# Attention weights times values in plain float32, two heads in two column halves of the array

## The chip, the cores and the metric

The kernel runs on one core of a Trainium2 chip. The metric is the device time of one execution in microseconds; three runs of the kernel before gave 1371.66 to 1372.84 us with a median of 1371.97. A core has a matrix engine (TensorE, in the profile PE, its weight loads PEld), a vector engine (DVE), a scalar engine (ACT), a general engine (POOL) and a queue engine that starts transfers (SP). They run side by side and wait for each other through semaphores.

## The reference

One step of a two-layer decoder: a retention layer, then a layer of sliding-window attention with grouped heads. There are 1024 prompt tokens and 8 decode tokens. The attention of the prompt, cut to what matters here:

```python
kk, vv = band(k), band(v)          # key blocks i-1 and i for query block i, 128 tokens each
scores = einsum('bnqkgd,bnskd->bnkgqs', qb, kk) * (SWA_HD ** -0.5)
scores = where(valid, scores - alibi_slopes() * dist, NEG)
p = sink_softmax(scores, sinks)    # softmax with one extra column per head, then dropped
o = einsum('bnkgqs,bnskd->bnqkgd', p, vv)
...
o = o * silu(gate)
return x + o @ w_out
```

There are 16 query heads of width 64 and 2 key/value heads, 8 query heads for each. A block of queries reads its own block of keys and the one before; the first block reads only its own. The change concerns the last product, `o`.

## The kernel before

The matrix engine multiplies a stationary operand (the weights, up to 128 rows by 128 columns) with a moving one, and adds up in PSUM. The kernel wants more precision than its fast float type, `float32r`, gives. So it splits most operands into a rounded part and the rest (`hi` and `lo`, both float32r) and adds three products: hi x hi, hi x lo, lo x hi. The rounded part is made by an ACT copy, the rest by a subtraction, mostly on DVE.

The program has these stages: the projections of the retention layer (to about 700 us with the retention itself), the retention layer's output projection (to about 909 us), keys and values of the attention layer (to about 955 us), the attention units (955 to 1280 us), and the rest of the output projection.

The keys and values are made per block of 128 tokens (`kv_mm`, `kv_ev`, `kv_tr`, `kv_kk`). `kv_ev` scales the values out of PSUM into `vvh` (rounded) and `vvl` (the rest). Both are kept for all eight blocks, 128 columns each, 64 per key/value head. For the last block a further copy, `vo`, is made and written to an output.

A unit of attention is a pair of query heads and a block of queries: 8 pairs by 8 blocks make 64 units. They share out into groups of 3, 3 and 2 blocks (`TG`). A unit has four steps:

- `att_s`: four products of queries and keys (two heads, hi and lo of the keys) into `sc`, then bias, maximum and exponential (DVE, ACT).
- `att_r`: the reciprocal of the sum (DVE) and the scaling of the weights (POOL).
- `att_x`: the weights are transposed on PE in blocks of 128 by 128, four of them in a unit (two in the first block of a sequence, which has one key block), into a PSUM tile `tr` with the columns [key block][head][query]. ACT copies them, rounded, to `pth`, DVE subtracts to get `ptl`.
- `att_o`: the products with the values into the PSUM tile `o`, of which there is one. Its 64 partitions hold the width of a head, its 256 columns are the 128 queries of head 0 and those of head 1. ACT copies each half, times 0.5, into its half of the partitions of `ot`, and POOL multiplies by the gate `gt`.

Around these steps, `fill` puts pieces of the projections of queries and gates (`pair_proj`, lines L1090 to L1092, 384 or 264 columns each), so that PE has other work while the other engines do the softmax of a unit. The main loop at the end of `_trunk` sets this order: `att_s` and `att_r` of unit m+4, a piece of projection, `att_x` of unit m+1, another piece, `att_o` of unit m, another piece. PE runs in exactly the order in which the code is written; for DVE, ACT, POOL and SP the order behind the first units is made by a scheduler from the dependences.

Other lines that the text below speaks of: L1430 and L1432 are small plain float32 products of squares with `hsel` for the norm of the queries (L1432 only in the last group of a pair, with 2 columns of weights); L1601 and L1606 are the scores of the decode tokens, plain float32 with 16 columns of weights; L1643 and L1645 their products with the values; L1380 copies transposed keys of the cache; L103 is the helper of all transposes.

Of the kernel before, what the change touches and what calls it, by code (L numbers as in the profile page):

```python
# [7 lines left out]
F32 = mybir.dt.float32  # L8
F32R = mybir.dt.float32r
AF = mybir.ActivationFunctionType  # L10
ALU = mybir.AluOpType
# [52 lines left out]
def trunk(tc, x_prompt, x_sample, state_ret, cache_k, cache_v, norm_ret, w_in_ret, ret_out_norm,  # L64
          w_out_ret, norm_swa, w_in_swa, q_norm, k_norm, sinks, w_out_swa, c1, c2,
          y_p, y_s, nrp, nrs, nkp, nvp, nks, nvs):
    nc = tc.nc
    ctx = ExitStack()
    with ctx:
        ctx.enter_context(tc.manual_schedule(engines=MS))  # L70
        _trunk(ctx, tc, nc, locals())


def _trunk(ctx, tc, nc, a):
# [7 lines left out]
    nkp, nvp, nks, nvs = a["nkp"], a["nvp"], a["nks"], a["nvs"]  # L82
# [12 lines left out]
    mm = nc.tensor.matmul  # L95
# [6 lines left out]
    def tr(out, in_, ident, start=True, stop=True):  # L102
        nc.tensor.matmul(out, in_, ident, is_transpose=True, start=start, stop=stop)  # L103
# [501 lines left out]
    o = lambda fn, *a: (fn, a)  # L605
# [118 lines left out]
    for h in range(H):  # L724
        t0 = max(t0 + GAP, sets[3 * h + 2].end + 10.0)
        for hf in range(2):
            for b in range(ND):
                d = {}
# [493 lines left out]
    o = 0  # L1222
# [23 lines left out]
    opp = ctx.enter_context(tc.tile_pool(name="opp", bufs=1, space=PSUM))  # L1246
    kvp = ctx.enter_context(tc.tile_pool(name="kvp", bufs=1))
    atp = ctx.enter_context(tc.tile_pool(name="atp", bufs=1))

    kkh = kvp.tile([128, 2, NP], F32R, name="kkh")  # L1250
    kkl = kvp.tile([128, 2, NP], F32R, name="kkl")
    vvh = kvp.tile([128, 8, 128], F32R, name="vvh")
    vvl = kvp.tile([128, 8, 128], F32R, name="vvl")
    kdd = kvp.tile([8, 128], F32, name="kdd")
    vdd = kvp.tile([8, 128], F32, name="vdd")
    rbc = kvp.tile([128, NT], F32, name="rbc")
# [4 lines left out]
    def knorm_a(src, r, n):  # L1261

        kj = atp.tile([128, HD], F32, tag="s", name="kj", bufs=6)
        ss = atp.tile([128, 2], F32, name="kss", bufs=2)
        rk = atp.tile([128, 2], F32, name="krk", bufs=2)
        for g in range(2):
            nc.scalar.activation(kj[:n], src[:, g * 64:g * 64 + 64], AF.Square, scale=r, accum_out=ss[:n, g:g + 1])
        nc.vector.tensor_scalar(ss[:n], ss[:n], 1.0 / HD, EPS, ALU.mult, ALU.add)
        rsq(rk[:n], ss[:n], 2)
        return rk  # L1270

    def knorm_b(out4, src, rk, r, n, dup):

        nc.vector.tensor_scalar(rk[:n], rk[:n], r, None, ALU.mult)
        for g in range(2):
            nc.vector.scalar_tensor_tensor(
                out4[:, g], src[:, g * 64:g * 64 + 64].unsqueeze(1).broadcast_to([n, dup, 64]), rk[:n, g:g + 1],
                kgb[:n].unsqueeze(1).broadcast_to([n, dup, 64]), ALU.mult, ALU.mult)
# [19 lines left out]
    def kv_ev(c):  # L1298
        ps = kvst[c]
        r = r9[:, c:c + 1]  # L1300
        nc.scalar.activation(vvh[:, c, :], ps[:, 128:256], AF.Copy, scale=r)
        rk = knorm_a(ps[:, 0:128], r, 128)
        nc.vector.scalar_tensor_tensor(vvl[:, c, :], ps[:, 128:256], r, vvh.bitcast(F32)[:, c, :],
                                       ALU.mult, ALU.subtract)
        kd = atp.tile([128, 2, 2, HD], F32, tag="s", name="kd", bufs=6)
        knorm_b(kd, ps[:, 0:128], rk, r, 128, 2)
        if c == 7:
            vo = atp.tile([128, 128], F32, tag="s", name="vo", bufs=6)
            nc.scalar.activation(vo, ps[:, 128:256], AF.Copy, scale=r)
            nc.scalar.dma_start(out=nvp[0, 0].rearrange("s g d -> s (g d)"), in_=vo)  # L1310
        kvst[c] = kd

    def kv_tr(c):
# [58 lines left out]
    def dec_cache(hf):  # L1372

        pt = trp.tile([128, 512], F32, name="tr")
        for i in range(4):
            tr(pt[:, i * 128:i * 128 + 128], kcT["c"][:, 4 * hf + i, :], ident)
        return pt
# [107 lines left out]
    for p_ in range(8):  # L1485
        for ti_, (t0_, t1_) in enumerate(TG):
            nch_ = (min(t1_, NP) - t0_) // 128
            for i_ in range(nch_):
                u = Unit()
# [48 lines left out]
    def att_x(u):  # L1538
        hs = (0, 1) if u.c > 0 else (1,)
        pt = trp.tile([128, 512], F32, name="tr")  # L1540
        for hf in hs:
            for j in range(2):
                tr(pt[:, hf * 256 + j * 128:hf * 256 + j * 128 + 128], u.st[:, j, hf * 128:hf * 128 + 128], ident)
        a0 = hs[0] * 256
        pth = atp.tile([128, 512], F32R, name="pth", bufs=2)
        ptl = atp.tile([128, 512], F32R, name="ptl", bufs=2)
        nc.scalar.activation(pth[:, a0:], pt[:, a0:], AF.Copy)
        nc.vector.tensor_tensor(ptl[:, a0:], pt[:, a0:], pth.bitcast(F32)[:, a0:], ALU.subtract)
        u.pt = (pth, ptl)

    def att_o(u):
        p, ti, i, c = u.p, u.ti, u.i, u.c
        if i == 0:
            ots[p, ti] = atp.tile([128, 384], F32, name="ot", bufs=2)
        ot, gt = ots[p, ti], G[p, ti]
        hs = (0, 1) if c > 0 else (1,)
        pth, ptl = u.pt
        po = opp.tile([64, 256], F32, tag="o", name="o")
        vs = slice(u.g * 64, u.g * 64 + 64)
        for hf in hs:  # L1560
            kc = c - 1 + hf
            rs_ = slice(hf * 256, hf * 256 + 256)
            mm(po, vvh[:, kc, vs], pth[:, rs_], start=(hf == hs[0]), stop=False)
            mm(po, vvl[:, kc, vs], pth[:, rs_], start=False, stop=False)
            mm(po, vvh[:, kc, vs], ptl[:, rs_], start=False, stop=(hf == 1))
        cs = slice(i * 128, i * 128 + 128)
        for j in range(2):
            nc.scalar.activation(ot[j * 64:j * 64 + 64, cs], po[:, j * 128:j * 128 + 128], AF.Copy, scale=0.5)
        nc.gpsimd.tensor_tensor(ot[:, cs], ot[:, cs], gt[:, cs], ALU.mult)
        if i == u.nch - 1:  # L1570
            done["o"] += 1
            n = u.nch * 128
            if p < 7:
                nc.scalar.dma_start(out=oscr[p, :, u.t0:u.t0 + n], in_=ot[:, :n])
            else:
                ts_ = slice(u.t0, u.t0 + n)
                nc.scalar.activation(A_hi[:, 7, ts_], ot[:, :n], AF.Copy)
                nc.vector.tensor_tensor(A_lo[:, 7, ts_], ot[:, :n], A_hif[:, 7, ts_], ALU.subtract)
                oready[ti] = True
# [118 lines left out]
    def so_all():  # L1698
        order = [(ft, ti) for ti in range(3) for ft in range(6)] + [(ft, ti) for ft in (6, 7) for ti in range(3)]
        early = []  # L1700

        def start(ft, ti):
            so_ahead(ft // 2 + 1)
            t0, t1 = TG[ti]
            n = t1 - t0
            xr = iop2.tile([128, 384], F32, tag="xr", bufs=2, name="xr2")
            nc.sync.dma_start(out=xr[:, :n], in_=xscr[ft, :, t0:t1])
            nso[0] += 1
            ps = (msp.tile([128, 512], F32, tag="ms", name="pm") if nso[0] % 3 == 0 else
                  pjp.tile([128, 512], F32, tag="pj", name="pj"))  # L1710
            for k in range(7):
                proj(ps[:, :n], so_slots[ft // 2], ft % 2, t0, t1, first=(k == 0), last=False, ks=[k])
                yield 3 * n / 2400.0
            early.append((ft, ti, ps, xr))

        def finish():
            ft, ti, ps, xr = early.pop(0)
            t0, t1 = TG[ti]
            n = t1 - t0
            proj(ps[:, :n], so_slots[ft // 2], ft % 2, t0, t1, first=False, last=True, ks=[7])  # L1720
            yield 3 * n / 2400.0
            yt = io("sq", 2)
            nc.vector.tensor_tensor(yt[:, :n], ps[:, :n], xr[:, :n], ALU.add)
            if pend_y:
                so_y(*pend_y.pop(0))
            pend_y.append((ft, ti, yt))

        for ft, ti in order:
            while early and (oready[early[0][1]] or len(early) == 3):
                while not oready[early[0][1]]:  # L1730
                    yield 1e9
                yield from finish()
            while ti == 2 and not oready[2]:
                yield 1e9
            yield from start(ft, ti)
        while early:
            yield from finish()
        while pend_y:
            so_y(*pend_y.pop(0))
# [6 lines left out]
    def stream():  # L1746
        for p in range(8):
            yield from pair_proj(p)

    ps = stream()  # L1750
    ones = atp.tile([128, 128], F32, tag="s", name="ones", bufs=6)
    nc.gpsimd.memset(ones, 1.0)
    out = so_all()
# [49 lines left out]
    pt = dec_cache(0)  # L1803
# [5 lines left out]
    pt = dec_cache(1)  # L1809
# [10 lines left out]
    fill(ps, 3.0)  # L1820
    att_r(units[3])
    att_x(units[0])
    sk.close()
    src = ps
# [8 lines left out]
    for m in range(NU):  # L1833
        u = units[m]
# [66 lines left out]
```

## Time and profile before

| | |
|---|---|
| three runs, median (lowest, highest) | 1371.97 us (1371.66, 1372.84) |
| profiled execution, span from the first to the last instruction | 1368.6 us |
| mean granted clock of TensorE | 0.987 |
| attention units, stretch 955 to 1280 us: PE busy | 316.16 of 325 us |
| products of `att_o`: records in the trace | 3 x 120, 128 rows x 64 columns of weights, 256 columns moving |
| DVE, `ptl` | 56 of 686 ns, 8 of 412 ns |
| ACT, `pth` | 56 of 595 ns, 8 of 367 ns |
| ACT, `ot` | 128 of 266 ns |

The page of a profile describes one execution. Its times are in microseconds where not marked ns. A group of instructions is written as line, engine, operation, output<-inputs, shapes, count | busy time, mean ns of one | idle time of the engine just before them, and what ended it. A timeline row is the start, the time that the row covers, the engine, the line and the operation, with neighbouring equal instructions merged (x4). Matmuls are pipelined: the recorded duration of one reaches past the start of the next, so the distance from start to start is what one costs in a stream.

### The profile page before, as it was taken

To read this page: it belongs to the slowest core of one execution; us is meant where nothing else is said; L and a number is where in the kernel's file an instruction comes from. 1 tells how busy PE (TensorE), PEld (TensorE's weight loads), DVE (VectorE), ACT (ScalarE), POOL (GpSimd) and SP (SyncE) were. 2 spreads that over 40 slices of the span, in tenths; PEclk is the share of its full clock that TensorE was granted. 3 is DMA by queue.
4 is the path that set the end of the run, shared out by engine and by line. 5 is a ranking of instruction groups with operands and counts; after the bars stand their busy time and mean duration, and the time that the engine had idled before them with its cause. 6 is when DMAs were issued, how large, how long until landed. Compare 5 with 4: busy or idle time off the path is not lost.

```text
span 1368.6 us, 25998 instructions
## 1 busy us (share of the span) xinstructions
PE 1313.7 (96%) x9541; PEld 1251.6 (91%) x9541; DVE 745.5 (54%) x1434; ACT 669.1 (49%) x1690; POOL 760.5 (56%) x886
## 2 busy tenths in 40 slices
PE   6999999999999999897979999998999999999998
PEld 6999999999999999686868889997899999998998
DVE  6943665566556553675752112335576777779321
ACT  5532555555556653675741112244576666667311
POOL 6753656655566753697976553544476666544000
PEclk9999999999999999999989999999999999999999
DMA  6314767667667653665645344442111111112532
GB/s 218 103 59 143 220 211 230 176 214 231 199 215 209 219 156 93 188 176 191 172 150 164 123 154 125 135 131 66 47 50 59 44 47 41 40 34 88 170 84 82
DMA packets 192804, 186.66 MB, mean 136 GB/s; under 512 B 12725, under 2 KB 172525, under 8 KB 192661
## 3 DMA queue, kind: packets, MB, share of 16 engines
q1 hardware_dynamic: 155840, 148.87, 35.9%
q10 hardware_dynamic: 36836, 36.14, 8.3%
q8 instruction: 75, 1.23, 0.4%
q14 instruction: 53, 0.43, 0.1%
HBM read 128.59 MB, written 57.41 MB: 136 GB/s over the span
## 4 chain that ended last, share of the span: by engine, by line
PE 84%; DVE 5%; POOL 4%; DMA 3%; issue 2%; ACT 2%; SPq 0%; ACTq 0%; POOLq 0%; DVEq 0%
PE b L340 7%; PE b L342 7%; PE b L341 7%; PE pj L1090 5%; PE pj L1091 5%; PE pj L1092 5%; PE pj L1141 4%; PE pj L1139 4%; PE pj L1140 4%; PE b L334 4%; PE b L333 4%; PE b L335 4%; PE tr L103 3%; PE S L921 1%; PE S L922 1%
## 5 line engine op out<-in xcount | busy, mean ns | idle before, releaser
L340 PE MATMUL b<-xh,woh 128*128 128x258 f32 x784 | 222.4, 284 | 0.0
L342 PE MATMUL b<-xh,wol 128*128 128x258 f32 x784 | 221.9, 283 | 0.0
L341 PE MATMUL b<-xl,woh 128*128 128x258 f32 x784 | 221.6, 283 | 0.0
L1090 PE MATMUL pj<-A_hi,wh 128*128 128x384 f32 (+1 forms) x512 | 173.0, 338 | 0.0
L1091 PE MATMUL pj<-A_lo,wh 128*128 128x384 f32 (+1 forms) x512 | 165.7, 324 | 0.0
L1092 PE MATMUL pj<-A_hi,wl 128*128 128x384 f32 (+1 forms) x512 | 165.5, 323 | 0.0
L340 PEld LDWEIGHTS b<-xh,woh 128*128 128x128 f32 x784 | 148.2, 189 | 1.2
L341 PEld LDWEIGHTS b<-xl,woh 128*128 128x128 f32 x784 | 148.8, 190 | 0.0
L342 PEld LDWEIGHTS b<-xh,wol 128*128 128x128 f32 x784 | 148.2, 189 | 0.0
L1080 POOL TENSOR_TENSOR wl<-wr,wh 128x1024 fp32r<-128x1024 f32 (+1 forms) x60 | 114.8, 1924 | 46.4 <-DVE wh L1079 22.1
L334 PE MATMUL b<-wol,xh 128*128 128x256 f32 x448 | 126.1, 282 | 1.2 <-DVE wol L224 1.2
L333 PE MATMUL b<-woh,xh 128*128 128x256 f32 x448 | 125.9, 281 | 0.0
L335 PE MATMUL b<-woh,xl 128*128 128x256 f32 x448 | 125.8, 281 | 0.0
L1536 POOL TENSOR_TENSOR s<-s,sm 128x512 f32<-128x512 f32 x64 | 67.7, 1057 | 69.2 <-DVE sm L1535 67.5
L282 POOL TENSOR_TENSOR yl<-yd,yh 128x256 fp32r<-128x256 f32 x64 | 56.3, 879 | 82.0 <-PE od L289 40.3
L1090 PEld LDWEIGHTS pj<-A_hi,wh 128*128 128x128 f32 x512 | 98.0, 191 | 0.2
L1091 PEld LDWEIGHTS pj<-A_lo,wh 128*128 128x128 f32 x512 | 98.0, 191 | 0.0
L1092 PEld LDWEIGHTS pj<-A_hi,wl 128*128 128x128 f32 x512 | 97.4, 190 | 0.0
L224 POOL TENSOR_TENSOR wol<-raw,woh 128x512 fp32r<-128x512 f32 x52 | 68.8, 1331 | 47.8 <-ACT woh L219 46.9
L334 PEld LDWEIGHTS b<-wol,xh 128*128 128x128 f32 x448 | 84.4, 188 | 1.4 <-DVE wol L224 1.4
L333 PEld LDWEIGHTS b<-woh,xh 128*128 128x128 f32 x448 | 84.4, 188 | 0.7
L335 PEld LDWEIGHTS b<-woh,xl 128*128 128x128 f32 x448 | 84.4, 188 | 0.0
(368 smaller groups left out, 3847.0 us busy)
## 6 DMA issues: line engine op xcount, KB each, us to landing
raw<-in_w_in_ret_dram ACTq DMA_DIRECT2D x44, 512.0 KB
st<-in_state_ret_dram SPq DMA_DIRECT2D x64, 256.0 KB
out_dram<-st SPq DMA_DIRECT2D x64, 256.0 KB
wr<-in_w_out_ret_dram SPq DMA_DIRECT2D x32, 512.0 KB
wr<-in_w_in_swa_dram SPq DMA_DIRECT2D x18, 512.0 KB
vb<-vscr SPq DMA_DIRECT2D x64, 128.0 KB
evp<-qks SPq DMA_DIRECT2D x32, 256.0 KB
evx<-vsc SPq DMA_DIRECT2D x32, 256.0 KB
```

The costliest lines, as they stand in the source:

```text
L224: eng.tensor_tensor(lo, src_of(s, name, sub), hi.bitcast(F32), SUB)
L333: mm(dst, xh, wh, start=a and i == 0, stop=False, skip_group_check=True)
L334: mm(dst, xh, wl, start=False, stop=False, skip_group_check=True)
L335: mm(dst, xl, wh, start=False, stop=z, skip_group_check=True)
L340: mm(dst, wh, xh, start=a, stop=False, **sg)
L341: mm(dst, wh, xl, start=False, stop=False, **sg)
L342: mm(dst, wl, xh, start=False, stop=z, **sg)
L1080: lo_eng[0].tensor_tensor(lo[:, js, :], raw[:, i:i + step, :], hi.bitcast(F32)[:, js, :], ALU.subtract)
L1090: mm(ps, hi[:, k, fs], xh[:, k, t0:t1], start=first and k == ks[0], stop=False)
L1091: mm(ps, hi[:, k, fs], xl[:, k, t0:t1], start=False, stop=False)
L1092: mm(ps, lo[:, k, fs], xh[:, k, t0:t1], start=False, stop=last and k == ks[-1])
L1536: nc.gpsimd.tensor_tensor(st[:, :, 0:256], st[:, :, 0:256], sm.unsqueeze(2).broadcast_to([128, 2, 256]), ALU.mult)
```

## The change

The values are kept once, in plain float32 (`vv`), and the transposed weights too (`ptf`). The subtractions that made `vvl` and `ptl` are gone, and so is the extra copy of the last block's values, whose output is now written from `vv`. In `att_o` each key block is multiplied separately for the two heads, with the same 64 columns of values as weights: head 0 writes partitions 0 to 63 of `o`, head 1 partitions 64 to 127. So `o` has 128 partitions and 128 columns, and one ACT copy takes it to `ot`. In the built program the products of `att_o` are marked, before as now, with a tile of 128 rows by 64 columns of the array; before all of them at column 0, now head 0 at column 0 and head 1 at column 64.

```diff
-    vvh = kvp.tile([128, 8, 128], F32R, name="vvh")
-    vvl = kvp.tile([128, 8, 128], F32R, name="vvl")
+    vv = kvp.tile([128, 8, 128], F32, name="vv")
...
-        nc.scalar.activation(vvh[:, c, :], ps[:, 128:256], AF.Copy, scale=r)
+        nc.scalar.activation(vv[:, c, :], ps[:, 128:256], AF.Copy, scale=r)
         rk = knorm_a(ps[:, 0:128], r, 128)
-        nc.vector.scalar_tensor_tensor(vvl[:, c, :], ps[:, 128:256], r, vvh.bitcast(F32)[:, c, :],
-                                       ALU.mult, ALU.subtract)
...
-            vo = atp.tile([128, 128], F32, tag="s", name="vo", bufs=6)
-            nc.scalar.activation(vo, ps[:, 128:256], AF.Copy, scale=r)
-            nc.scalar.dma_start(out=nvp[0, 0].rearrange("s g d -> s (g d)"), in_=vo)
+            nc.scalar.dma_start(out=nvp[0, 0].rearrange("s g d -> s (g d)"), in_=vv[:, 7, :])
...
-        pth = atp.tile([128, 512], F32R, name="pth", bufs=2)
-        ptl = atp.tile([128, 512], F32R, name="ptl", bufs=2)
-        nc.scalar.activation(pth[:, a0:], pt[:, a0:], AF.Copy)
-        nc.vector.tensor_tensor(ptl[:, a0:], pt[:, a0:], pth.bitcast(F32)[:, a0:], ALU.subtract)
-        u.pt = (pth, ptl)
+        ptf = u.pt = atp.tile([128, 512], F32, name="ptf", bufs=2)
+        nc.scalar.activation(ptf[:, a0:], pt[:, a0:], AF.Copy)
...
-        pth, ptl = u.pt
-        po = opp.tile([64, 256], F32, tag="o", name="o")
+        po = opp.tile([128, 128], F32, tag="o", name="o")
         vs = slice(u.g * 64, u.g * 64 + 64)
         for hf in hs:
-            kc = c - 1 + hf
-            rs_ = slice(hf * 256, hf * 256 + 256)
-            mm(po, vvh[:, kc, vs], pth[:, rs_], start=(hf == hs[0]), stop=False)
-            mm(po, vvl[:, kc, vs], pth[:, rs_], start=False, stop=False)
-            mm(po, vvh[:, kc, vs], ptl[:, rs_], start=False, stop=(hf == 1))
+            for j in range(2):
+                rs_ = slice(hf * 256 + j * 128, hf * 256 + j * 128 + 128)
+                mm(po[j * 64:j * 64 + 64, :], vv[:, c - 1 + hf, vs], u.pt[:, rs_], start=(hf == hs[0]), stop=(hf == 1))
         cs = slice(i * 128, i * 128 + 128)
-        for j in range(2):
-            nc.scalar.activation(ot[j * 64:j * 64 + 64, cs], po[:, j * 128:j * 128 + 128], AF.Copy, scale=0.5)
+        nc.scalar.activation(ot[:, cs], po, AF.Copy, scale=0.5)
```

How the instructions stand on PE around one unit before (a unit of the third pair of heads with two key blocks; `tr` are the transposes of the next unit, `pj` the projection):

```order
L1092 MATMUL pj<-A_hi,wl 128x384
L103 MATMUL tr<-ident,s 128x128 x4
L1563 MATMUL o<-pth,vvh 64x256
L1564 MATMUL o<-pth,vvl 64x256
L1565 MATMUL o<-ptl,vvh 64x256
L1563 MATMUL o<-pth,vvh 64x256
L1564 MATMUL o<-pth,vvl 64x256
L1565 MATMUL o<-ptl,vvh 64x256
L1090 MATMUL pj<-A_hi,wh 128x384
```

The same unit on PE after the change:

```order
L1091 MATMUL pj<-A_lo,wh 128x384
L1092 MATMUL pj<-A_hi,wl 128x384
L103 MATMUL tr<-ident,s 128x128 x4
L1554 MATMUL o<-ptf,vv 64x128 x4
L1090 MATMUL pj<-A_hi,wh 128x384
L1091 MATMUL pj<-A_lo,wh 128x384
```

Six products of 256 columns have become four of 128, in the same place; nothing else on PE has moved, in any unit.

On ACT, around a later unit of the fourth pair before (`s,sm` is the exponential, `gt` the gate, the DMA writes a finished group of `ot`):

```order
L1568 ACTIVATE ot<-o 64x128 x2
L1547 ACTIVATE pth<-tr 128x512
L1528 ACTIVATE s,sm<-s,mx 128x257 x2
L1454 ACTIVATE gt<-sq 128x384
L1568 ACTIVATE ot<-o 64x128 x2
L1574 DMA oscr<-ot 128x384
```

And after:

```order
L1556 ACTIVATE ot<-o 128x128
L1541 ACTIVATE ptf<-tr 128x512
L1523 ACTIVATE s,sm<-s,mx 128x257 x2
L1449 ACTIVATE gt<-sq 128x384
L1556 ACTIVATE ot<-o 128x128
L1562 DMA oscr<-ot 128x384
```

The two copies of a unit's result have become one; the order of the rest is the same here. On DVE the subtractions L1548 and L1303 are gone and their neighbours move up; on POOL the scaling of one unit's weights and the gating of another's result swap places in a number of units; on SP one load of `xr` moves ahead of a reload in the output projection, and another ahead of a weight load.

## The prediction

> **What bounds the kernel now.** I read the page first: the busy shares, the slices over time and the chain that ended last.
>
> ```profile
> span 1368.6 us, 25998 instructions
> PE 1313.7 (96%) x9541; PEld 1251.6 (91%) x9541; DVE 745.5 (54%) x1434; ACT 669.1 (49%) x1690; POOL 760.5 (56%) x886
> PEclk9999999999999999999989999999999999999999
> PE 84%; DVE 5%; POOL 4%; DMA 3%; issue 2%; ACT 2%; SPq 0%; ACTq 0%; POOLq 0%; DVEq 0%
> ```
>
> TensorE (PE) is busy for 96% of the span, at nearly the full clock, and holds 84% of the chain. A mean can hide a stage with another limit, so next I cut out the stage that the change touches: the 64 attention units run between 955 and 1280 us. The view by windows has one row for all of it and one for its middle.
>
> ```profile
> 955.00:1280.00 325.00, 316.16 (x2272) 308.67 (x2271) 230.80 (x496) 210.62 (x611) 186.39 (x264) 0.99 0.18 56
> 1040.00:1240.00 200.00, 199.97 (x1454) 197.05 (x1452) 148.59 (x318) 135.73 (x402) 118.54 (x172) 1.00 0.14 43
> ...
> PE pm L1430 <- ACT sq L1409: 4.8, 2, 2.5
> PE o L1563 <- ACT ot L1568: 1.6, 2, 1.3
> PE sc L1601 <- DVE s L1524: 1.4, 2, 1.2
> PE o L1643 <- ACT ot L1568: 0.6, 1, 0.6
> PE o L1565 <- DVE ptl L1548: 0.3, 1, 0.3
> ```
>
> The columns after the window and its length are PE, weight load, DVE, ACT, POOL. In the 200 us of the middle PE is busy for 199.97 us while DVE has 148.59, ACT 135.73 and POOL 118.54: nothing else limits. The rows below the dots are all that PE waited for in the stage (total, times, longest): 8.7 us. So every microsecond that the change adds to or takes from PE's own stream moves the end by nearly as much, and work taken from DVE and ACT can give back at most those 8.7 us.
>
> **How the products run now.** The timeline of PE and of its weight loads (PEld) around one unit:
>
> ```profile
> 1106.91 0.34 PE L1092 MATMUL pj<-A_hi,wl 128*128 128x384 f32 x1
> 1107.09 0.28 PE L1563 MATMUL o<-pth,vvh 128*64 128x256 f32 x1
> ...
> 1107.67 0.28 PE L1565 MATMUL o<-ptl,vvh 128*64 128x256 f32 x1
> 1107.79 0.33 PE L1090 MATMUL pj<-A_hi,wh 128*128 128x384 f32 x1
> 1107.96 0.34 PE L1091 MATMUL pj<-A_lo,wh 128*128 128x384 f32 x1
> ...
> 1106.91 0.14 PEld L1563 LDWEIGHTS o<-pth,vvh 128*64 128x64 f32 x1
> 1107.21 0.13 PEld L1565 LDWEIGHTS o<-ptl,vvh 128*64 128x64 f32 x1
> ```
>
> The durations overlap; what counts is the distance between starts. Six products take 1107.79 - 1107.09 = 0.70 us, 0.117 each. The step from the 384-column projection into them is 0.18, as between two projections (0.17), and the step out is 0.12: going from a 128-wide to a 64-wide weight and back costs nothing here. The weight load of the first product starts with the matmul ahead of it (both 1106.91).
>
> **The change, term one: the products themselves.** Six float32r products of 256 columns become four plain float32 products of 128 columns. How plain float32 runs, the decode scores (L1601) show, and L1606 and L1430 show pairs of load and matmul that stream almost nothing:
>
> ```profile
> L1601 PE MATMUL sc<-acc,Qd 128*16 128x128 f32 x16 | 2.1, 276 | 1.4 <-DVE s L1524 1.4
> L1606 PEld LDWEIGHTS tr<-kdT,Qd 128*16 128x16 f32 x16 | 0.7, 115 | 0.0
> ...
> 1251.90 1.06 PE L1601 MATMUL sc<-acc,Qd 128*16 128x128 f32 x8 [1.16 <-DVE s L1524]
> 1252.80 0.66 PE L1606 MATMUL tr<-kdT,Qd 128*16 128x1 f32 x16
> ...
> 1252.69 0.68 PEld L1606 LDWEIGHTS tr<-kdT,Qd 128*16 128x16 f32 x16
> 1253.39 0.42 PEld L103 LDWEIGHTS tr<-ident,s 128*128 128x128 f32 x4
> ...
> 1111.61 0.76 PEld L1430 LDWEIGHTS pm<-C,sq 128*128 128x128 f32 x6
> 1112.28 0.19 PEld L1090 LDWEIGHTS pj<-A_hi,wh 128*128 128x128 f32 x1
> ```
>
> The program has 8 products at L1601 and the trace 16 records: a plain float32 product is two passes, each with its own weight load. Eight passes of 128 columns last 1.06 us and the last of them 0.276, so one follows another every (1.06 - 0.276)/7 = 0.112 us. A unit will therefore have 8 passes of 0.112 where it had 6 of 0.117. One behind the other that is 0.90 us against 0.70. The two passes of one product share their columns of the array and must follow each other; the second pass of head 0 and the first of head 1 have different columns and different output partitions, so they may overlap. No row of before shows two matmuls in different columns, so I bound the step between them: 0.112 above (no overlap), 0 below. Between these, the weights: the load at 1106.91 starts with the matmul ahead of it and not before, and pairs of load and matmul follow each other at (0.68 - 0.115)/15 = 0.038 us with 16 columns of weights (L1606) and (0.76 - 0.19)/5 = 0.114 with 128 (L1430). On the line between, 64 columns give 0.038 + 48/112 x 0.076 = 0.070. I take 0.070, since it is the price for this width. The eight passes then last 5 x 0.112 + 3 x 0.070 = 0.77 us (inner steps 0.112, between heads 0.070, the last pass in full): +0.07 against 0.70. In the 8 units of the first block (one key block, four passes) it is 3 x 0.112 + 0.070 = 0.41 against 3 x 0.117 = 0.35: +0.06.
>
> **Term two: going in and out of the narrow shape.** The only plain float32 product with narrow weights amid the attention stream is L1432 (2 columns):
>
> ```profile
> 967.45 0.61 PE L1430 MATMUL pm<-C,sq 128*128 128x2 f32 x4 [2.54 <-ACT sq L1409]
> 967.99 0.20 PE L1432 MATMUL pm<-sq,C 128*2 128x8 f32 x2
> 968.11 0.44 PE L1090 MATMUL pj<-A_hi,wh 128*128 128x384 f32 x1
> 968.39 0.34 PE L1091 MATMUL pj<-A_lo,wh 128*128 128x384 f32 x1
> ...
> 967.45 0.52 PEld L1430 LDWEIGHTS pm<-C,sq 128*128 128x128 f32 x4 [2.86 <-ACT sq L1409]
> 967.99 0.09 PEld L1432 LDWEIGHTS pm<-sq,C 128*2 128x2 f32 x2
> 968.11 0.19 PEld L1090 LDWEIGHTS pj<-A_hi,wh 128*128 128x128 f32 x1
> ```
>
> The last load of L1430 starts at 967.45 + 0.52 - 0.19 = 967.78, the first of L1432 0.21 later; where L1430 is followed by a 128-wide float32r product the distance is 0.10 (1111.61 + 0.76 - 0.19 = 1112.18, then 1112.28). So 0.10 more on the way in. On the way out the second matmul of L1432 starts at 967.99 + 0.20 - 0.17 = 968.02, and the next load not with it, as elsewhere, but at 968.11; L1091 at 968.39 less a step of 0.17 puts L1090's real start at 968.22, 0.20 behind. The same 0.10 stands behind L1606 (its last matmul at about 1253.29, the next load at 1253.39). I read this as: the array empties for 0.10 us, and only then the next weights are loaded, in the open. A unit pays in: 0.10 plus a load of 64 columns, 0.07; out: 0.10 plus a load of 128 columns, 0.11; together 0.38 us, and 64 x 0.38 = 24.3 us. The other end is the 64-wide float32r products above, which pay nothing: 0. I take 0.38, since the new products are plain float32 as at L1432, not float32r.
>
> The Trainium skill, "TensorEngine Tiling (Array Packing)", Key Properties, says that changing the tiling mode drains the engine and that changing only the tile does not. The trace agrees at L1432 and not at L1563, which has 64-wide weights and no gap. By that rule alone both kernels would switch 128 times, nothing would be added, and the sum below would end at 1372.4 us; by the rows it ends at 1396.7. The skill's "PSUM — Partial Sum Buffer", The four PSUM rules, mentions that float32r matmuls force the full column mask, which would reconcile the two; no run here shows it.
>
> **Term three: what DVE and ACT lose.**
>
> ```profile
> L1548 DVE TENSOR_TENSOR ptl<-tr,pth 128x512 fp32r<-128x512 f32 x56 | 38.4, 686 | 5.7 <-ACT pth L1547 4.1
> L1568 ACT ACTIVATE ot<-o 64x128 f32<-64x128 f32 x128 | 34.0, 266 | 8.4 <-PE o L1565 7.1
> L1547 ACT ACTIVATE pth<-tr 128x512 fp32r<-128x512 f32 x56 | 33.3, 595 | 37.6 <-PE tr L103 30.6 <-POOL s L1517 6.6
> L1380 ACT ACTIVATE acc<-tr 128x512 f32<-128x512 f32 x2 | 1.2, 585 | 0.0
> ```
>
> DVE loses the subtraction (38.4 us and the small ones of the first blocks), ACT one of two evacuations of 266 ns per unit, 17 us; the copy to plain float32 costs what the rounding copy did (585 against 595 ns). None of it is on PE's path in the middle. It can shorten PE's waits: those behind `ot` and `ptl` (1.6 + 0.6 + 0.3) I count as gone, and a third of the wait for `sq` (1.5): -4.0 us, between 0 and -8.7. In the key/value part 8 small subtractions and one copy go; the chain there runs over the normalisation of the keys, which stays: 0. On SP's and POOL's queues nothing is added; a few neighbours swap places, and both have slack (POOL 118.54 of 200 us): 0.
>
> **Sum.** 56 x (0.07 + 0.38) + 8 x (0.06 + 0.38) = 25.2 + 3.5 = 28.7, less 4.0: +24.7 us. The profiled span of 1368.6 becomes 1393.3; the runs lie 3.4 us above the span (median 1371.97), so 1396.7 us.
>
> **Rivals.**
> - *The halves don't run side by side at all* (the change doesn't do what its words say): step 0.112. 56 x (0.196 + 0.38) + 8 x (0.098 + 0.38) - 4.0 = +32.1, 1404 us. For it: no row shows an overlap. Against: nothing but the separate columns.
> - *They overlap fully*: step 0, so a unit's passes last 5 x 0.112 = 0.56. 56 x (-0.14 + 0.38) + 8 x (-0.014 + 0.38) - 4.0 = +12.4, 1384 us. Still slower, because the switches outweigh it. The Trainium skill, "TensorE: Matmul & The Clock Gate", Part 3, has matmuls in distinct column groups start some 4 ns apart, which would give an estimated 1385; no run here shows it yet.
> - *Faster: the switch costs nothing*, as at L1563. Then the passes decide: with step 0, 56 x (-0.14) - 8 x 0.014 - 4.0 = -11.9, 1360 us; with 0.070 it is 4.4 - 4.0, 1372.4. It is faster when the step stays below about 0.068 (176 x step < 12), and by more than the bound below 0.053, and both gaps at the border are gone. For it: the 64-wide rows of the same lines. Against: the three gaps behind L1430, L1432 and L1606.
>
> **Chances.** My forecast 0.34, no overlap 0.27, full or nearly full overlap 0.23, no switch cost 0.12 (0.08 of it faster, 0.03 within the bound, 0.01 slower), the rest 0.04. The bound is 0.2%, 2.7 us, about what a measurement of this kernel can tell from no change. Faster 0.09, same 0.04, slower 0.87. The range takes in the first three cases with a margin of 2 to 5 us for the size of the switch and for the waits: 1382 to 1409.
>
> **What would show it.** In the timeline of the changed kernel, around one unit: two records per product at 0.112; a first record of head 1 that starts 0.070 behind the second of head 0 (0.112 or 0 for the rivals); the first weight load of the unit about 0.10 behind the end of the projection ahead, not at its start; some 0.3 us from the last pass to the next projection. The forecast is wrong if the loads go on starting with the matmul ahead (no switch cost), or if PE in the middle window waits for ACT or DVE.

## The result, and the profile after

Twenty runs of the changed kernel have a median of 1369.98 us (1367.17 to 1374.43), twenty of the kernel before 1370.73 (1367.02 to 1372.84). The ratio is 0.9997 with a 95% interval of 0.9989 to 1.0005: no change that can be measured. The forecast was +1.8%.

Of the page of the changed kernel, the span and the busy shares:

```profile
span 1369.9 us, 26110 instructions
PE 1318.6 (96%) x9661; PEld 1235.3 (90%) x9661; DVE 708.4 (52%) x1362; ACT 651.4 (48%) x1625; POOL 762.7 (56%) x886
```

The attention stage by windows, and all that PE waited for in it:

```profile
955.00:1280.00 325.00, 319.77 (x2378) 292.12 (x2376) 196.89 (x432) 193.01 (x547) 186.15 (x263) 0.98 0.18 54
1040.00:1240.00 200.00, 200.00 (x1516) 183.47 (x1515) 121.75 (x267) 120.59 (x350) 116.74 (x171) 1.00 0.13 38
...
PE pm L1425 <- ACT sq L1404: 4.5, 2, 2.5
PE sc L1589 <- DVE s L1519: 0.8, 2, 0.4
PE o L1631 <- ACT ot L1556: 0.4, 1, 0.4
```

DVE fell from 148.59 to 121.75 us in the middle window and ACT from 135.73 to 120.59; PE is as full as before. Its waits in the stage fell from 8.7 to 5.7 us. One unit with two key blocks, first PE and then its weight loads; the last row is the same group seen through a window of 0.02 us:

```profile
1110.44 0.33 PE L1092 MATMUL pj<-A_hi,wl 128*128 128x384 f32 x1
1110.71 0.66 PE L1554 MATMUL o<-ptf,vv 128*64 128x128 f32 x8
1111.30 0.45 PE L1090 MATMUL pj<-A_hi,wh 128*128 128x384 f32 x1
1111.58 0.34 PE L1091 MATMUL pj<-A_lo,wh 128*128 128x384 f32 x1
...
1110.27 0.19 PEld L1092 LDWEIGHTS pj<-A_hi,wl 128*128 128x128 f32 x1
1110.71 0.42 PEld L1554 LDWEIGHTS o<-ptf,vv 128*64 128x64 f32 x8 [0.25 <-issue]
1111.29 0.19 PEld L1090 LDWEIGHTS pj<-A_hi,wh 128*128 128x128 f32 x1 [0.17 <-issue]
...
1110.71 0.33 PE L1554 MATMUL o<-ptf,vv 128*64 128x128 f32 x2
```

Two things are to be seen. First, the gaps at the borders are there: the first load of the unit starts at 1110.71, 0.27 us behind the start of L1092 and so 0.10 behind the end of its step of 0.17; the weight path stands idle for 0.25 and 0.17 us where nothing but issue is named. Second, the eight passes take 0.66 us with the last one's own 0.27, so their starts lie within 0.39 us. Two of them start within 0.01 us of each other (the last row: two records in 0.33 us, the length of one that waits for its weights). The passes run in four pairs, about 0.11 us from pair to pair. I read a pair as one pass of each head; the records do not name the head, and the first experiment tests it.

From the start of L1092 to the real start of the next projection (1111.58 less a step of 0.17) the unit takes 0.97 us; before it took 1107.79 - 1106.91 = 0.88. In a unit of the first block it was 0.53 before and is 1101.21 - 0.17 - 1100.30 = 0.74 now (two rows of before, three of after):

```profile
983.25 0.34 PE L1092 MATMUL pj<-A_hi,wl 128*128 128x384 f32 x1
983.78 0.34 PE L1090 MATMUL pj<-A_hi,wh 128*128 128x384 f32 x1
```

```profile
1100.30 0.34 PE L1092 MATMUL pj<-A_hi,wl 128*128 128x384 f32 x1
1100.56 0.44 PE L1554 MATMUL o<-ptf,vv 128*64 128x128 f32 x4
...
1101.21 0.34 PE L1091 MATMUL pj<-A_lo,wh 128*128 128x384 f32 x1
```

So PE's own stream grew by 56 x 0.09 + 8 x 0.21 = 6.7 us. The last product of the stage started at 1276.7 us before and at 1279.8 now, 3.1 later, with 3.0 us of waits less (the last start in each row, before and then after):

```profile
L1565 PE MATMUL o<-ptl,vvh x120: 276/279/416, 983.7 to 1276.7; 128*64 128x256 f32 x120
L1554 PE MATMUL o<-ptf,vv x480: 272/273/477, 984.1 to 1279.8; 128*64 128x128 f32 x160
```

What follows the last product took 1368.6 - 1276.7 = 91.9 us before and 90.1 now. The windows differ in the clock, before and then after:

```profile
1270.00:1290.00 20.00, 19.36 (x120) 18.63 (x119) 7.62 (x16) 7.75 (x19) 0.92 (x2) 0.91 0.49 142
```

```profile
1270.00:1290.00 20.00, 19.62 (x141) 18.05 (x136) 8.12 (x16) 8.25 (x19) 1.38 (x3) 1.00 0.48 140
```

The granted clock (third number from the right) was 0.91 in that window before and is 1.00 now. That accounts for the 1.8 us between these two executions, but it can't be put down to the change: the run "Head by head" below has the same waits of PE there as the changed kernel (0.8 us behind `s`, 0.4 behind `ot`), and its profile shows 0.83 in the same window:

```profile
1270.00:1290.00 20.00, 19.61 (x118) 18.20 (x116) 6.24 (x13) 6.96 (x16) 0.92 (x2) 0.83 0.45 135
```

What the copies cost is as forecast (596 and 268 ns):

```profile
L1541 ACT ACTIVATE ptf<-tr 128x512 f32<-128x512 f32 x56 | 33.4, 596 | 52.7 <-PE tr L103 42.8 <-POOL s L1512 9.7
L1556 ACT ACTIVATE ot<-o 128x128 f32<-128x128 f32 x64 | 17.1, 268 | 6.0 <-PE o L1554 5.7
```

### The profile page after: what moved, and what is told of

The parts are those of the page before. It is cut to its first block, busy times and chain, and to the rows that moved or that the text cites. A ratio compares the mean times of both kernels' runs of the same rounds, so it can differ in the third digit from the quotient of the medians.

```text
span 1369.9 us, 26110 instructions
## 1 busy us (share of the span) xinstructions
PE 1318.6 (96%) x9661; PEld 1235.3 (90%) x9661; DVE 708.4 (52%) x1362; ACT 651.4 (48%) x1625; POOL 762.7 (56%) x886
## 4 chain that ended last, share of the span: by engine, by line
PE 87%; DVE 4%; POOL 3%; DMA 2%; issue 2%; ACT 1%; SPq 0%; ACTq 0%; POOLq 0%; DVEq 0%
PE b L340 7%; PE b L342 7%; PE b L341 7%; PE pj L1090 6%; PE pj L1091 6%; PE pj L1092 6%; PE pj L1141 4%; PE pj L1139 4%; PE pj L1140 4%; PE b L334 4%; PE b L333 4%; PE b L335 4%; PE tr L103 4%; PE o L1554 2%; PE tr L862 1%
## 5 line engine op out<-in xcount | busy, mean ns | idle before, releaser
L1090 PE MATMUL pj<-A_hi,wh 128*128 128x384 f32 (+1 forms) x512 | 178.6, 349 | 0.0
L1092 PE MATMUL pj<-A_hi,wl 128*128 128x384 f32 (+1 forms) x512 | 165.1, 323 | 0.0
L1092 PEld LDWEIGHTS pj<-A_hi,wl 128*128 128x128 f32 x512 | 97.1, 190 | 0.0
```

The source lines that it names most:

```text
L1090: mm(ps, hi[:, k, fs], xh[:, k, t0:t1], start=first and k == ks[0], stop=False)
L1092: mm(ps, lo[:, k, fs], xh[:, k, t0:t1], start=False, stop=last and k == ks[-1])
```

## The experiments

The theory that the profile after suggests: the two heads run side by side, pass by pass, which makes the products cheaper than they were; the borders take that back; the relief of DVE and ACT pays the rest. Each run changes one part of it. Times are set against runs of the kernel before on the same chip; the changed kernel stands at a ratio of 0.9997.

### Both heads in one column half

```diff
-        po = opp.tile([128, 128], F32, tag="o", name="o")
+        po = opp.tile([64, 256], F32, tag="o", name="o")
...
-                mm(po[j * 64:j * 64 + 64, :], vv[:, c - 1 + hf, vs], u.pt[:, rs_], start=(hf == hs[0]), stop=(hf == 1))
+                mm(po[:, j * 128:j * 128 + 128], vv[:, c - 1 + hf, vs], u.pt[:, rs_], start=(hf == hs[0]), stop=(hf == 1))
...
-        nc.scalar.activation(ot[:, cs], po, AF.Copy, scale=0.5)
+        for j in range(2):
+            nc.scalar.activation(ot[j * 64:j * 64 + 64, cs], po[:, j * 128:j * 128 + 128], AF.Copy, scale=0.5)
```

The loop over the heads also stands outside the loop over the key blocks here.

> The four products of a unit as changed, but both heads write the same 64 partitions, next to each other in columns, so both use one column half of the array; two copies take them out, as before the change. Theory (the two halves run side by side, pass by pass; a unit pays 0.35 us at its borders and 0.11 us per pair of passes): the eight passes follow each other at 0.11, 0.44 us more in each of 56 units and 0.22 in 8, +26 us against the changed kernel, about 1396 us. Rival (plain float32 of 64 columns is simply quicker than in the decode scores, side by side or not): as the changed kernel, 1370 us, with starts 0.055 apart.

Measured: 1393.07 us, ratio 1.0177 (1.0150 to 1.0205), 1.8% more than the changed kernel's ratio, 24.7 us. The rows of a unit on PE:

```profile
1107.93 0.34 PE L1092 MATMUL pj<-A_hi,wl 128*128 128x384 f32 x1
1108.20 1.09 PE L1554 MATMUL o<-ptf,vv 128*64 128x128 f32 x8
1109.21 0.44 PE L1090 MATMUL pj<-A_hi,wh 128*128 128x384 f32 x1
```

Eight passes of the same shape need 1.09 us instead of 0.66, (1.09 - 0.27)/7 = 0.117 from start to start. The gap ahead of them is the same 0.27. The rival falls: without two halves a pass costs what it cost in the decode scores. The products alone account for the difference, 0.43 x 56 + 0.21 x 8 = 25.8 us (0.21 is what a unit of the first block takes longer), so the second copy on ACT, which this kernel also has, is not needed to explain it.

### Head by head

```diff
-        for hf in hs:
-            for j in range(2):
+        for j in range(2):
+            for hf in hs:
```

> As changed, but the products are written head by head: head 0 with both key blocks, then head 1. Theory A (the engine takes the next pass of the other half from further back in its queue): as the changed kernel, 1370 us, starts in pairs. Theory B (only neighbours in the order of the program overlap): the four passes of head 0 run alone but for the last, three more steps of 0.11 in 56 units, +18 us, 1388 us.

Measured: 1369.46 us, ratio 0.9997 (0.9986 to 1.0009).

```profile
1107.38 0.33 PE L1092 MATMUL pj<-A_hi,wl 128*128 128x384 f32 x1
1107.64 0.66 PE L1554 MATMUL o<-ptf,vv 128*64 128x128 f32 x8
...
1107.64 0.34 PE L1554 MATMUL o<-ptf,vv 128*64 128x128 f32 x2
```

The same 0.66 us for eight passes. Theory B falls, and with it the way in which the forecast had counted. In the order of this program the four passes of head 0 stand ahead of those of head 1, and yet they run side by side. Either the engine takes them out of order, or a step behind the program that I can see has mixed the heads. The records speak for the first. In the changed kernel the first two passes of a unit start 6 to 7 ns apart, in all 64 units. Here it is 13 to 14 ns in all 56 units with two key blocks (0.34 us for the two records in the last row, against 0.33 above) and again 6 to 7 ns in the 8 units of the first block, where both programs have the same order. So the partner starts twice as far behind where twice as many passes stand between the two, as if the engine reached that much further back in its queue; a stream with the heads already mixed would be expected to look like that of the changed kernel. This is argued from the starts: the order of the instructions at the engine was not read out. What is said further up, that PE runs in exactly the order of the code, does not hold for the starts of these passes.

### Four borders instead of two

```diff
         for hf in hs:
+            if hf == 1 and c > 0:
+                fill(src, 0.1)
             for j in range(2):
```

> As changed, but a piece of projection (three matmuls, 128 wide, taken from those that follow) stands between the products of the two key blocks, so a unit with two key blocks has four borders between wide and narrow instead of two. No work is added. Theory (a pair of borders costs 0.35 us): 56 x 0.35 = +20 us, about 1390 us. Rival (the borders are free or hidden, and the result came out even because the products cost what they did): 1370 us.

Measured: 1389.15 us, ratio 1.0142 (1.0121 to 1.0162): 0.0145 above the changed kernel, 19.9 us. A split unit, and behind the dots one that was not split:

```profile
1106.86 0.34 PE L1092 MATMUL pj<-A_hi,wl 128*128 128x384 f32 x1
1107.13 0.44 PE L1556 MATMUL o<-ptf,vv 128*64 128x128 f32 x4
1107.50 0.44 PE L1090 MATMUL pj<-A_hi,wh 128*128 128x384 f32 x1
1107.78 0.33 PE L1091 MATMUL pj<-A_lo,wh 128*128 128x384 f32 x1
1107.95 0.34 PE L1092 MATMUL pj<-A_hi,wl 128*128 128x384 f32 x1
1108.22 0.44 PE L1556 MATMUL o<-ptf,vv 128*64 128x128 f32 x4
...
1129.08 0.66 PE L1556 MATMUL o<-ptf,vv 128*64 128x128 f32 x8
```

Each half unit now has its own 0.27 us between L1092 and the products. From L1092 to the real start of the next projection it takes 1107.78 - 0.17 - 1106.86 = 0.75 us; less the projection's 0.17 and two pairs of passes at 0.11 this leaves 0.36 us for a pair of borders. The rival falls, and the price of the borders, argued from three places in the forecast, is shown by the rows.

The total does not show it as well as it seems to. In the trace only 39 of the 56 units are split; in the other 17 `fill` had no matmul to give and the eight passes still stand together. So the extra borders make 39 x 0.36 = 14.0 us, and that the sum for 56 units met the measured 19.9 is luck. Of the other 6 us, with an interval of some 3 us either way, PE's waits in the stage hold 2.2 (7.9 against 5.7); the rest was not taken apart.

### Plain float32 at full width

```diff
-        po = opp.tile([128, 128], F32, tag="o", name="o")
+        po = opp.tile([128, 256], F32, tag="o", name="o")
...
+            rs_ = slice(hf * 256, hf * 256 + 256)
+            mm(po, vv[:, c - 1 + hf, :], u.pt[:, rs_], start=(hf == hs[0]), stop=(hf == 1))
...
+        for j in range(2):
+            nc.scalar.activation(ot[j * 64:j * 64 + 64, cs], po[vs, j * 128:j * 128 + 128], AF.Copy, scale=0.5)
```

> Plain float32 with 128 columns of weights (the values of both key/value heads; the half that the unit doesn't need is computed too and left unused), 256 columns moving, no column halves. Theory (the border gap belongs to the narrow shape): four passes of 256 columns at 0.22 = 0.87 us without borders, against 0.44 + 0.35 = 0.79 in the changed kernel, +0.08 x 56 - 0.14 x 8 = +3 us, about 1373 us. Rival (the gap belongs to plain float32 of any width): 0.87 + 0.35, +24 us, 1394 us.

Measured: 1376.44 us, ratio 1.0048 (1.0029 to 1.0067), 7 us above the changed kernel.

```profile
1108.31 0.34 PE L1092 MATMUL pj<-A_hi,wl 128*128 128x384 f32 x1
1108.48 1.02 PE L1553 MATMUL o<-ptf,vv 128*128 128x256 f32 x4
1109.52 0.34 PE L1091 MATMUL pj<-A_lo,wh 128*128 128x384 f32 x1
```

The products follow the projection at 0.17 us, without a gap: plain float32 of full width has no border, so the rival falls. The unit takes 1109.52 - 0.17 - 1108.31 = 1.04 us against 0.97. That is 0.07 x 56 = 3.9 us; less the first blocks' gain this is the +3 expected. The measured 7 holds some 4 us more. A second copy per unit on ACT, which this kernel needs, may hold a part: PE waits 3.0 us for `ot` in the stage, against 0.4 in the changed kernel. The rest was not taken apart.

### DVE and ACT keep their old load

```diff
+        ptl = atp.tile([128, 512], F32R, name="ptl", bufs=2)
+        nc.vector.tensor_tensor(ptl[:, a0:], pt[:, a0:], ptf[:, a0:], ALU.subtract)
...
-        nc.scalar.activation(ot[:, cs], po, AF.Copy, scale=0.5)
+        for j in range(2):
+            nc.scalar.activation(ot[j * 64:j * 64 + 64, cs], po[j * 64:j * 64 + 64, :], AF.Copy, scale=0.5)
```

> As changed, but DVE still makes the subtraction (of the same size, its result unused) and ACT still takes the result out in two copies. Theory (PE alone sets the stage; the relief of DVE and ACT shortens only a few waits): 0 to +4 us against the changed kernel, 1370 to 1374 us. Rival (it is the relief that paid for the borders): +7 us or more, 1377 us.

Measured: 1375.67 us, ratio 1.0042 (1.0030 to 1.0055): 0.0045 above the changed kernel, 6 us. It lies between what the two expected. The load is back (first two rows); the two longest new waits of PE and the windows of the last units show where it counts:

```profile
L1543 DVE TENSOR_TENSOR ptl<-tr,ptf 128x512 fp32r<-128x512 f32 x56 | 38.4, 685 | 9.2 <-ACT ptf L1541 7.7
L1559 ACT ACTIVATE ot<-o 64x128 f32<-64x128 f32 x128 | 34.2, 267 | 6.0 <-PE o L1556 4.7
...
PE sc L1516 <- DVE rbc L1593: 2.5, 1, 2.5
PE sc L1592 <- DVE s L1519: 2.2, 2, 1.2
...
1250.00:1270.00 20.00, 16.51 (x121) 14.79 (x122) 16.84 (x34) 11.56 (x32) 6.20 (x7) 0.91 0.15 47
1270.00:1290.00 20.00, 18.51 (x124) 16.68 (x123) 9.38 (x18) 8.68 (x22) 2.36 (x4) 0.91 0.41 126
```

The changed kernel has in the first of these windows

```profile
1250.00:1270.00 20.00, 19.23 (x159) 16.49 (x159) 19.15 (x38) 12.87 (x36) 9.46 (x11) 1.00 0.25 79
```

Between 1250 and 1290 us PE is busy for 35.0 of 40 us here, at a clock of 0.91; in the changed kernel it is 38.9, at 1.00. There the decode scores' chain on DVE (`rbc`) meets the softmax of the last units, and PE waits. In the middle window PE is as full as in the changed kernel (200.00 of 200 us). So the relief was worth 6 us, some 4 to 8 by the intervals, and what the traces show of it is shorter waits near the end: 9.9 us in the stage here against 5.7. The clock does not explain the rest: over the whole profiled execution it is 0.990 here and 0.987 in the changed kernel.

### Half the borders, and a quarter

`att_o` takes two units (or four) at once: their products stand next to each other, `o` holds 128 columns for each, and one (or three) more buffers hold the transposed weights.

```diff
-        att_o(u)
+        batch.append(u)
+        if len(batch) == (2 if m < 64 else 1):
+            att_o(batch)
+            batch = []
```

> As changed, but the products of two units stand next to each other (the first waits for the second), so there are 32 pairs of borders instead of 64; one more buffer of transposed weights. Theory: -32 x 0.35 = -11 us against the changed kernel, about 1359 us. Rival (the borders are free or hidden): 1370 us. Second rival (the later results of every other unit make PE wait): above 1362 us with new waits in the stage.

Measured: 1368.9 us, ratio 0.9990 (0.9981 to 0.9999): 1 us under the changed kernel, no more than the intervals leave open, where 11 were expected.

> As the run with pairs, but four units together for the first 56 units and single ones for the last 8: 22 pairs of borders instead of 64. Theory: -42 x 0.35 = -15 us against the changed kernel, about 1355 us. Rivals as for the pairs: 1370 us, or above 1360 us with new waits.

Measured: 1384.76 us, ratio 1.0112 (1.0096 to 1.0127): 16 us over it. The rows of the pairs and, behind the dots, of the fours:

```profile
L1552 PE MATMUL o<-ptf,vv x480: 272/273/324, 987.0 to 1274.2; 128*64 128x128 f32 x160
PE o L1552 <- ACT ptf L1541: 2.9, 1, 2.9
PE o L1635 <- ACT ot L1560: 1.7, 1, 1.7
1270.00:1290.00 20.00, 18.26 (x105) 17.49 (x105) 6.47 (x13) 6.83 (x16) 1.52 (x2) 0.83 0.38 112
```

```profile
PE pm L1425 <- ACT sq L1404: 19.6, 8, 7.2
1040.00:1240.00 200.00, 189.17 (x1446) 183.02 (x1447) 108.27 (x256) 113.63 (x336) 109.06 (x164) 0.97 0.11 34
```

With pairs the last product starts at 1274.2 us, 5.6 ahead of the changed kernel's 1279.8. One of the two new waits stands ahead of it: the 2.9 us for `ptf` are over at 1245.17 us, right before the products of unit 57 (of 0 to 63). The other, 1.7 us for `ot`, is over at 1276.21, and the end behind the last product takes 94.6 us instead of 90.1, at a clock of 0.83 in the window. The gain was given back in these two places; that is the second rival. How much of the end is the clock's is open, since "Head by head" has 0.83 there too, without the waits, and takes 1370.2 - 1277.0 = 93.2 us. With fours the wait moves into the stage itself: PE waits 19.6 us for `sq`, the squares of the queries, up to 7.2 at a time, and the middle window is no longer full. The projections that fill the gaps are held back by a count of finished units, which now rises in steps of four; that this is the cause is argued from the code and was not tried apart.

So the pairs were tried with single units at the end, from unit 56 and from unit 48 on (`2 if m < 56`, `2 if m < 48`).

> Products of two units next to each other for the first 56 units, single ones for the last 8. In the run with pairs throughout, the stretch from the first to the last product was 8.5 us shorter than in the changed kernel, but PE then waited 4.6 us for the transposed weights and results of the last units and ran part of the end at half clock. Theory (the gain is real and is given back only by the last units): 28 x 0.35 = 9.8 us less than the changed kernel, about 1360 us, end as in the changed kernel. Rival (the waits move with the last pair): about 1368 us, as with pairs throughout.

Measured: 1366.63 us, ratio 0.9973 (0.9958 to 0.9988), 3 us under the changed kernel, where 9.8 were expected. A wait of 2.8 us for `ot` (L1552 <- L1560) ends at 1244.41 us, ahead of unit 57, where the pairs throughout had their 2.9: single units from 56 on leave that wait in place. The 8.5 us of the expectation also held 2.9 us by which the first product starts later with pairs (987.0 against 984.1).

> The same, with single units from unit 48 on, before the output projection begins to fill the gaps. Theory: 24 x 0.35 = 8.4 us less than the changed kernel, about 1362 us. Rival: about 1368 us.

Measured: 1363.25 us, ratio 0.9960 (0.9945 to 0.9974), 5 us under the changed kernel by the ratios and the best of all; the profile has

```profile
L1552 PE MATMUL o<-ptf,vv x480: 272/273/324, 987.5 to 1270.0; 128*64 128x128 f32 x160
PE pm L1425 <- ACT sq L1404: 4.2, 2, 2.5
1270.00:1290.00 20.00, 19.62 (x126) 19.11 (x123) 7.05 (x14) 6.90 (x16) 0.45 (x1) 1.00 0.65 192
```

The last product starts at 1270.0 us, 9.8 ahead of the changed kernel, the end takes 90.1 us again, and of the waits for the copies 0.4 us is left, as in the changed kernel. The two profiled executions flatter it, though (1362.29 us, below the median here, and 1371.73, above it there): by the ratios 5 of the 8.4 us expected came. The saving of a border per two units is real where waits do not take it back; its full size is not shown by the times.

## Why the prediction was wrong

The bound was read rightly: PE's own stream decided the stage, and no transfer or queue came into it. The result lies outside the range because of one term above all.

**Term one, the products: this is the step that failed.** The forecast had the passes of a unit start in the order of the program, so that only the last pass of one head could overlap the first of the other, and gave 0.77 us for eight of them. Even its lower bound, full overlap, was counted that way: five steps, 0.56 us. The runs show four steps: the heads run in lockstep from their first pass on, two passes for 0.11 us. With a unit's 0.97 us less the projection's 0.17 and the border's 0.36, 0.44 us are left for the eight passes. Against 0.70 before that is -0.26 where +0.07 stood. Over all units: PE's stream grew by 6.7 us; with 64 x 0.36 = 23.0 for borders the products themselves gave back 16.3, where the forecast had +4.4. This is 20.7 us of the 25 by which it missed. One half of the array instead of two costs 24.7 us, head by head instead of in turns costs nothing: both speak for the same reading. The interpolation by the width of the weights (0.070) rested on rows with a single column group, in which each load waits for the matmul ahead; with two groups the eight loads take 0.42 us, and 0.85 in one (1108.19 in the run with one half).

```profile
1108.19 0.85 PEld L1554 LDWEIGHTS o<-ptf,vv 128*64 128x64 f32 x8 [0.25 <-issue]
```

The Trainium skill, "TensorE: Matmul & The Clock Gate", Part 3, says that matmuls in different tiles of the array run at once, with some 4 ns for each further tile, and that packing by columns comes within some 5 ns of packing by rows. The trace agrees: two starts within 0.01 us. It says as well that matmuls start in the order of the program; by that, unless a later step has mixed the heads, the run with the heads outside would have been slower, and it was not. The measurement decides, and its 13 to 14 ns speak against such a step. The forecast had taken the first sentence for a rival and the second, unsaid, for its arithmetic.

**Term two, the borders: right.** 0.38 us for a unit was forecast, 0.36 read in the timeline, in whole units and in split ones, 23.0 us in all against 24.3. The choice between the two rows of before, the narrow float32r products without a gap and the narrow plain float32 ones with it, went the right way. "TensorEngine Tiling (Array Packing)", Key Properties, of the Trainium skill has the drain without a size; here it is 0.10 us on either side, and the loads that it uncovers make up the rest: 0.05 us on the way in (0.32 us for the first record, 0.27 for a later one) and 0.11 on the way out (1111.29 to 1111.40 for the next load).

**Term three, the relief: right in sign, its size open.** -4.0 us were counted (bounds 0 and -8.7); putting the load back costs 6, some 4 to 8 by the intervals, while the list of PE's waits shrank by 3.0. What makes up the difference was not taken apart.

Together, with the 6: 24.7 less 20.7, 1.3 and 2.2 makes +0.5 us; measured were -0.4, with an interval of -1.5 to +0.7.

**The rivals.** *No overlap* (1404) was run as such: 1393. The borders were a little cheaper there too; what else makes up the 11 us was not taken apart. *Full overlap* (1384) came nearest, but it let only the last pass of one head meet the first of the next, and the runs show every pass with a partner: 1370. *No switch cost* fell. The signs named in advance did their work: the loads 0.10 us behind the projection's end and 0.3 us from the last pass to the next projection came as said. The start of head 1 came as none had it: with the first pass of head 0, not with or behind its second.

## What to carry to other kernels

Two products with 64 columns of weights in the two column halves of the array can cost as much as one, even in plain float32, whatever their order in the program; but each stretch of such narrow products in a stream of full-width ones cost 0.36 us here, so they gain by standing in long ones. When a price must lie between two bounds, ask whether the bounds rest on an assumption about order that no row shows; mine did, and the truth lay below both. And before products are gathered into longer stretches, look who waits for the last of them: two units together gained 1 us, and 5 once the last sixteen units were left single.

## What the hardware showed that was not expected

- Eight passes of plain float32 in two column halves: starts within 0.39 us; in one half 0.82 us. Their weight loads pair up too (0.42 against 0.85 us).
- The order of the heads in the program made no difference to the time (ratio 0.9997 both times); the start of the partner moved from 6 to 7 ns to 13 to 14 ns.
- Narrow float32r products have no gap at their borders (steps 0.18 and 0.12 us), narrow plain float32 ones 0.36 us in all, full-width plain float32 ones none (0.17).
- Near the end of the stage (1270 to 1290 us) the granted clock was 0.91 before, 1.00 in the changed kernel and 0.83 in "Head by head", whose waits there are those of the changed kernel. One profile of each kernel can't price a change by that window.
